# A hybrid decoder block on one core: both branch projections by seven products, the attention gate applied at the operand's load, transfers begun a set number of products ahead

## The chip, the core and the metric

The kernel runs on one core of a Trainium2 chip. The metric is the device time in microseconds, the median of several runs. Before the change it is 926.31 us (three runs, 925.58 to 927.93). A trace of one execution of the same kernel, taken by the hardware profiler, is what the numbers below are read from. Five engines work side by side, each through its own list of instructions in order: TensorE (PE, matrix products, with its weight loads listed as PEld), VectorE (DVE), ScalarE (ACT), GpSimd (POOL), and SyncE (SP). SP does no arithmetic here, it issues transfers; POOL issues the transfers of weights.

## What is computed

One layer, 1024 tokens, model width 1024, in float32. The reference, cut to what matters:

```python
h = rms_norm(x, norm_g[l])
proj = jnp.einsum("bsd,de->bse", h, w_in[l])
# u, g_rnn, q, k, v, g_attn, m_rnn, m_attn are column ranges of proj
u = causal_depthwise_conv(u, conv_w[l], conv_b[l])
y_rnn = rg_lru(u, ...) * jax.nn.silu(g_rnn)
y_attn = sliding_window_attention_with_sinks(q, k, v, attn_sinks[l]) * jax.nn.silu(g_attn)
merged = (jax.nn.sigmoid(m_rnn) * jnp.einsum("bsr,rd->bsd", y_rnn, w_rnn_out[l])
          + jax.nn.sigmoid(m_attn) * jnp.einsum("bsa,ad->bsd", y_attn, w_attn_out[l]))
x = x + jnp.einsum("bsd,de->bse", merged, w_o[l])
return rms_norm(x, final_norm_g)
```

The change is about the two projections in `merged`, each a 1024x1024 matrix times a 1024x1024 one.

## The kernel before

Everything is held feature by token: a tile is 128 features by 512 tokens (half of the sequence). TensorE works on a float32 operand that ACT and DVE have cut into a rounded high part and a remainder: ACT casts (`h`), DVE subtracts (`l`), which is `split_buf` (lines L422 and L423). One float32 product of a 128x128 block with a 128x512 tile is then three matmuls: high by high, high by low, low by high. This text calls them three rows of PE.

**Pairs and seven products.** A unit of 128 output features over all 1024 inputs is one column block of a weight. Two units form a pair, and a pair is a 2x2 block matrix A (A11, A12, A21, A22, each 512 inputs by 128 outputs) times the 2x2 block matrix B of the input (halves of the features by halves of the tokens). Class `Pair` computes it by the scheme of Strassen and Winograd with seven block products in place of eight. It needs sums of the blocks of A (S1 to S4, made on DVE for each pair), sums of the blocks of B (T1 to T4, made once for all pairs), a copy on ACT and five additions on DVE behind the products (L430). A block product is four blocks of 128 features by three matmuls, so 12 rows of PE. The projections of `w_in` (units `ug` for the recurrence and its gate, `mr` and `ma` for the merge gates, `k`, `v`, `q`, and `ga` for the attention gate) are done so.

**The two branch projections** (`zr` for the recurrence, `za` for attention, four pairs each) are done by `z_pair`, with eight products a pair: each of the two output blocks of a pair goes over eight feature blocks for both halves of the tokens. Their operand B comes from DRAM through `whole_from` (tiles `Wr`, cut into `Wh`, `Wl`). For `zr` it is `yr_dr`, written by the recurrence. For `za` it is `yg_dr`: `gate_attn` takes the silu of the gate (tile `tga`), loads the attention's result from `ya_dr` (tile `yld`), multiplies on DVE, and writes the product to `yg_dr`. Behind a pair, `z_pair` loads the stored merge gate (tile `tz`, from `tm_r` or `tm_a`), multiplies it with the result in PSUM (L999), and for `za` adds the two branches. Then `w_o` (`WO`, again `whole_from`) and the merged tiles (`mh`, `ml`) feed the last projection, the rows named `o`.

**What sets the order.** No engine's order is written out by hand. `Plan` collects all operations with costs, dependencies and priorities and lays them out by a list scheduler, engine by engine; table `TUNE` holds priorities, numbers of buffers by class, and in `orders` the order of pairs and of the 32 attention steps (`a00` to `a37`). A transfer may also be made to follow, in the plan, a key such as `first26` ("the pair with number 26 has begun"); such a key orders the plan, it is no semaphore on the chip. On the chip a transfer waits for its place in SP's or POOL's list, for its data, and for the buffer that it fills.

Of the kernel before, what the change touches and what calls it, by code (L numbers as in the profile page):

```python
# [17 lines left out]
S = 1024  # L18
D = 1024
P = 128  # L20
# [12 lines left out]
    'm': (30, 6, 3),  # L33
# [3 lines left out]
    'zy': 5,  # L37
    'raw': 5,
# [3 lines left out]
    'B': 23,  # L42
    'psw': 79,
    'psk': 0,
    'Y': 21,
    'ld': 8,
    'lds': 17,
    'kv': 8,
    'kvs': 4,
    'qt': 2,  # L50
    'qts': 8,
    'P': 13,
    'AO': 22,
# [12 lines left out]
    'xof': 153,
# [271 lines left out]
def hybrid_block_kernel(ctx: ExitStack, tc: tile.TileContext, x, wall, wo, bd, vec, gfin,  # L338
# [16 lines left out]
                "P": (16, 0, 0, TUNE["P"]), "AO": (32, 0, 0, TUNE["AOs"]), "Y": (64, 0, 0, TUNE["Y"]), "zy": (TUNE["zy"], 0, 0, 0), "wo": (32, 0, 0, TUNE["Y"]), "ld": (TUNE["ld"], 0, 0, TUNE["lds"]),  # L355
# [89 lines left out]


    class Pair:
# [38 lines left out]
        def product(self, ps, a, b, start):  # L486
            h, l = self.factor(a)
            for k in range(4):
                bh, bl = self.comb(b)[k]

                def go(k=k, bh=bh, bl=bl):
                    w = slice(k * P, (k + 1) * P)
                    kw = {} if start else {"skip_group_check": True}
                    nc.tensor.matmul(ps.t, h.t[:, w], bh.t, start=start and k == 0, stop=False, **kw)  # L494
# [3 lines left out]
                PE(go, 3, [h, l, bh, bl], [ps])  # L498

        def p1(self):  # L500
            self.a, self.c1 = bank("pair"), slot("p1")
            self.product(self.a, "A11", "B11", True)
            ACT(lambda q: q.copy(self.c1.t, self.a.t), HF, [self.a], [self.c1, f"first{self.i}"])

        def p2(self):
            self.product(self.a, "A12", "B21", False)

        def run(self):
            self.p1()
# [433 lines left out]
    yg_dr = dr.tile([KT, P, S], F32, name="yg_dr")  # L943

    def gate_attn(p, C):

        for q in range(2):
            for h in range(2):
                e_ = p + 4 * q
                src = C[q][h]  # L950
                t = slot("tga")
                ACT(lambda e, t=t, src=src: e.activation(t.t, src.t, AF.Silu), HF, [src], [t], tset=SILU)
                y = load("ld", "yld")
                DMA(lambda y=y: y.t, lambda e_=e_, h=h: ya_dr[e_, :, HALF[h]], 1 << 18,
                    [(ya_dr, (e_, n)) for n in range(4 * h, 4 * h + 4)], [y])
                tt(t, t, y, MUL)
                DMA(lambda e_=e_, h=h: yg_dr[e_, :, HALF[h]], lambda t=t: t.t, 1 << 18, [t], [(yg_dr, (e_, h))])

    def whole_from(src, after, prio, cls):

        T = {}

        def get(k, h):
            if (k, h) not in T:
                raw, hi, l = load("zy", "Wr"), buf(cls, dt=F32R, name="Wh"), buf(cls, dt=F32R, name="Wl")
                ap, key = src(k, h)
                DMA(lambda: raw.t, ap, 1 << 18, key + after, [raw], prio)
                split_buf(hi, l, raw, prio)
                T[k, h] = (hi, l)
            return T[k, h]  # L970

        return get

    MG = {}

    def z_pair(a, p, i, comb):

        for q, names in enumerate((("A11", "A12"), ("A21", "A22"))):
# [9 lines left out]
            for k in range(KT):  # L988
                h, l = W[k // 4]
                w = slice(k % 4 * P, k % 4 * P + P)  # L990
                for hf in range(2):
                    bh, bl = comb(k, hf)
                    PE(lambda ps=ps[hf], h=h, l=l, w=w, bh=bh, bl=bl, k=k: three(ps, h, l, w, bh, bl, k == 0, k == KT - 1), 3,
                       [h, l, bh, bl], [ps[hf], f"first{i}"])
            for hf in range(2):
                t = load("P" if a == "r" else "ld", "tz")
                DMA(lambda t=t: t.t, lambda e_=e_, hf=hf: tm_dr[a][e_, :, HALF[hf]], 1 << 18,
                    [(tm_dr[a], (e_, hf)), f"first{i - p}"], [t], TUNE["ztl"])
                DVE(lambda v, t=t, src=ps[hf]: v.scalar_tensor_tensor(t.t, t.t, 1.0, src.t, op0=ADD, op1=MUL), HF, [t, ps[hf]], [t])  # L999
                if a == "r":  # L1000
                    MG[e_, hf] = t
                else:
                    tt(MG[e_, hf], MG[e_, hf], t, ADD)

# [6 lines left out]
    ids = [base[a] + p for a, p in (it for it in seq if len(it) == 2)]  # L1011
    ZC = {}

    def begun(a, p):
        return f"first{base[a] + p}"

    def run_pair(a, p):
        i = ids.index(base[a] + p)
        if a[0] == "z":
            if p == 0:  # L1020
                ZC[a] = whole_from(dram_mat(yr_dr if a == "zr" else yg_dr), [begun(*TUNE[a])], TUNE["comb"], "Y")
            z_pair(a[1], p, ids[i], ZC[a])
            return
# [20 lines left out]
    def dram_mat(m):  # L1044
        return lambda k, h: ((lambda: m[k, :, HALF[h]]), [(m, (k, h))])
# [23 lines left out]
    WO = whole_from(lambda k, h: ((lambda: wo[k * P : (k + 1) * P, HALF[h]]), []), [begun(*TUNE["wo"])], TUNE["comb"], "wo")  # L1069
# [11 lines left out]
    for q in range(2):  # L1081
        DMA(lambda q=q: gf_b[q].t, lambda q=q: gfin[HALF[q]].partition_broadcast(P), 1 << 18, [begun(*TUNE["wo"])], [gf_b[q]])
    for r in range(NB):
        xh = [load("xo", "xo") for _ in range(2)]
        for c in range(2):
            DMA(lambda c=c, xh=xh, r=r: xh[c].t, lambda c=c, r=r: x[r * P : (r + 1) * P, HALF[c]], 1 << 18,
                [begun(*TUNE["wo"])], [xh[c]], TUNE["xof"])
# [77 lines left out]
```

## Time and profile before

| what | value |
|---|---|
| median of three runs | 926.31 us |
| the profiled execution's own time | 928.33 us |
| its span, first to last instruction | 926.6 us |
| mean granted clock of TensorE | 0.992 |
| last projection of `w_in` ends, first row of `zr` | 653.2 us, 653.45 us |
| last row of `za` begins | 832.2 us |
| last row of `o` begins | 919.39 us |

The page gives for each engine its busy time, its share of the span and its instructions. A group of instructions is one line of the kernel with the tiles that it writes and reads, a count, the busy time with the mean duration of one, and the idle time ahead of them with the releaser that ended it. The timeline lists instructions by start and duration. On PE and DVE, durations of instructions that follow each other overlap, so the cost of one in a stream is the step from start to start, not its duration.

### The profile page before, as it was taken

What the parts mean: (1) busy time and instruction counts of PE and PEld (TensorE: products, weight loads), DVE (VectorE), ACT (ScalarE), POOL (GpSimd) and SP (SyncE); (2) the same over time, 40 slices, a digit from 0 to 9 for tenths busy, and PEclk for the clock granted to TensorE, in tenths of its full rate; (3) what the DMA queues carried; (4) which work ended last, traced back from release to release, by engine and by line L of the source; (5) the groups of instructions that cost most, each with busy time, mean ns of one, the idle gap of its engine ahead of it and who ended that gap; (6) DMA issues with size and microseconds to landing.
All of it is one profiled execution on the core that took longest, in us unless ns stands there. A gap on an engine that the chain in (4) does not pass through costs nothing. (4 is left out here: it accounts for less than half of the span.)

```text
span 926.6 us, 13014 instructions
## 1 busy us (share of the span) xinstructions
PE 896.5 (97%) x4184; PEld 739.7 (80%) x4184; DVE 684.4 (74%) x1427; ACT 569.3 (61%) x1176; POOL 72.8 (8%) x131
## 2 busy tenths in 40 slices
PE   4999999999999999999999999999899999999996
PEld 3778888877888888788888788888688888888885
DVE  6987999989977889887898699789622533366433
ACT  7646999578658796969988888998511300133000
POOL 2101010001100100110001000001200010000000
PEclk9999999999999999999999999999999999999999
DMA  9311224616742345356555476438961284131111
GB/s 325 108 52 58 67 78 127 177 36 213 216 151 69 103 107 171 105 167 173 171 164 163 104 196 206 120 117 271 399 252 46 71 296 161 40 115 46 51 63 46
DMA packets 86884, 129.76 MB, mean 140 GB/s; under 512 B 10656, under 2 KB 40224, under 8 KB 86816
## 3 DMA queue, kind: packets, MB, share of 16 engines
q1 hardware_dynamic: 77216, 97.47, 33.4%
q0 software_dynamic: 9600, 31.46, 11.3%
q8 instruction: 33, 0.54, 0.2%
q14 instruction: 35, 0.29, 0.1%
HBM read 87.21 MB, written 41.68 MB: 139 GB/s over the span
## 5 line engine op out<-in xcount | busy, mean ns | idle before, releaser
L413 POOL DMA_DIRECT2D A<-in_wall_dram x120 | 64.4, 538 | 654.6 <-PE pair L496 111.1
L554 PE MATMUL z<-Wh,zh 128*128 128x512 f32 x256 | 100.5, 393 | 1.7 <-ACT Wh L422 1.6
L555 PE MATMUL z<-Wl,zh 128*128 128x512 f32 x256 | 100.4, 392 | 0.5 <-DVE Wl L423 0.5
L556 PE MATMUL z<-Wh,zl 128*128 128x512 f32 x256 | 100.3, 392 | 0.0
L999 DVE SCALAR_TENSOR_TENSOR tz<-tz,z 128x512 f32<-128x512 f32 x32 | 21.9, 686 | 98.0 <-PE z L556 95.4
L423 DVE TENSOR_TENSOR wl<-S,wh 128x512 fp32r<-128x512 f32 x96 | 65.3, 684 | 9.4 <-ACT wh L422 9.0
L422 ACT CAST Wh<-Wr 128x512 fp32r<-128x512 f32 x48 | 28.2, 619 | 66.8 <-PE z L555 31.5
L422 ACT CAST wh<-S 128x512 fp32r<-128x512 f32 x96 | 58.4, 616 | 9.6 <-DVE S L430 4.5
L900 ACT ACTIVATE sm<-sm,nm 128x256 f32<-128x256 f32 (+1 forms) x128 | 62.1, 489 | 0.0
L554 PEld LDWEIGHTS z<-Wh,zh 128*128 128x128 f32 x256 | 48.5, 189 | 12.6 <-ACT Wh L422 2.6
L555 PEld LDWEIGHTS z<-Wl,zh 128*128 128x128 f32 x256 | 48.5, 189 | 11.3 <-DVE Wl L423 1.2
L893 DVE CUSTOM_DVE_ANT_0 sm<-ps_s,mask_t,sink_t 128x256 f32<-128x256 f32 (+1 forms) x128 | 53.8, 459 | 4.9 <-PE ps_s L885 4.9
L422 ACT CAST mh<-tz 128x512 fp32r<-128x512 f32 x16 | 9.1, 618 | 78.2 <-DVE tz L430 78.2
L556 PEld LDWEIGHTS z<-Wh,zl 128*128 128x128 f32 x256 | 48.4, 189 | 10.0
L908 ACT ACTIVATE sm<-sm,dn 128x256 f32<-128x256 f32 (+1 forms) x128 | 53.3, 487 | 4.0 <-DVE dn L905 3.8
L549 ACT ACTIVATE sd<-ss,eps_t 128x1 f32<-128x1 f32 x16 | 4.3, 289 | 78.4 <-DVE ss L547 78.4
L423 DVE TENSOR_TENSOR wl<-A,wh 128x512 fp32r<-128x512 f32 x72 | 49.1, 682 | 4.5 <-ACT wh L422 4.5
L430 DVE TENSOR_TENSOR c<-pair,u 128x512 f32<-128x512 f32 x72 | 49.0, 682 | 3.7 <-PE pair L496 3.3
L555 PE MATMUL o<-Wl,mh 128*128 128x512 f32 x128 | 49.8, 389 | 0.0
L554 PE MATMUL o<-Wh,mh 128*128 128x512 f32 x128 | 49.8, 389 | 0.0
L556 PE MATMUL o<-Wh,ml 128*128 128x512 f32 x128 | 49.8, 389 | 0.0
L885 PE MATMUL ps_s<-K,qt 128*128 128x256 f32 (+1 forms) x288 | 43.4, 289 | 3.1 <-DMA qt<-st_q 2.6
(221 smaller groups left out, 2566.0 us busy)
## 6 DMA issues: line engine op xcount, KB each, us to landing
A<-in_wall_dram POOLq DMA_DIRECT2D x120, 256.0 KB, 3.5
qt<-st_q SPq DMA_DIRECT2D x32, 256.0 KB, 3.6
xt<-in_x_dram SPq DMA_DIRECT2D x16, 256.0 KB, 5.4
A<-in_wall_dram SPq DMA_DIRECT2D x16, 256.0 KB, 5.4
tm_r<-tm SPq DMA_DIRECT2D x16, 256.0 KB, 2.1
yr_dr<-tg SPq DMA_DIRECT2D x16, 256.0 KB, 2.1
K<-st_k SPq DMA_DIRECT2D x32, 128.0 KB, 3.5
st_q<-qh SPq DMA_DIRECT2D x32, 128.0 KB, 3.2
```

Of the source, the lines that this page charges most:

```text
L413: pl.op([("POOL", 1000.0)], reads, writes, lambda e: nc.gpsimd.dma_start(dst(), src()), prio, move=move)
L422: ACT(lambda e: e.copy(h(), src()), cols, reads, wh, prio)
L423: (DVE if psum else EW)(lambda e: e.tensor_tensor(l(), src(), h().bitcast(F32), op=ALU.subtract), cols, list(reads) + list(wh), wl, prio)
L430: (eng or EW)(lambda e: e.tensor_tensor(dst.t, a.t, b.t, op=op), HF, [a, b], [dst], prio)
L554: nc.tensor.matmul(ps.t, h.t[:, w], bh.t, start=start, stop=False)
L555: nc.tensor.matmul(ps.t, h.t[:, w], bl.t, start=False, stop=False)
L556: nc.tensor.matmul(ps.t, l.t[:, w], bh.t, start=False, stop=stop)
L885: nc.tensor.matmul(ps.t[:, j, o0 : o0 + pw], qt.t[:, h, :], K[m, half].t[:, c0 : c0 + pw], start=m == 0, stop=m == 1)
L893: DVE(lambda v, ps=ps, j=j, h=h, s=s: v.tensor_tensor_reduce(s.t[:, j, :], ps.t[:, j, :], att["mask"].t[:, 256 - w : 256], scale=-0.125, s ...
L900: ACT(lambda e, h=h, s=s, j=j: e.activation(s.t[:, j, :], s.t[:, j, :], AF.Exp, scale=-1.0, bias=nm.t[:, h : h + 1], accum_out=dn.t[:, h : ...
L908: ACT(lambda e, h=h, s=s, j=j: e.activation(s.t[:, j, :], s.t[:, j, :], AF.Identity, scale=dn.t[:, h : h + 1]), w, [(s, j), dn], [(s, j)], ...
L999: DVE(lambda v, t=t, src=ps[hf]: v.scalar_tensor_tensor(t.t, t.t, 1.0, src.t, op0=ADD, op1=MUL), HF, [t, ps[hf]], [t])
```

## The change

1. **Seven products for the branches.** `zr` and `za` go through `Pair` (in `z_seven`), as the other projections do. Their operands come from `comb_from`, which loads 16 raw tiles of a branch (class `Y`), makes T1 to T4 (16 subtractions on DVE), and cuts seven blocks of four tiles into high and low parts (28 casts, 28 subtractions), where `whole_from` cut 16 tiles.
2. **The attention gate at the load.** `gate_attn` takes the silu and writes it to a new array `sg_dr`; it no longer loads `ya_dr`, multiplies, or writes `yg_dr`. In its place `fetch` loads for each tile of `za`'s operand both `ya_dr` and `sg_dr` (tile `zg`, three buffers) and multiplies on DVE.
3. **Keys by products.** Every product of a pair now leaves a key ("product 217"), and transfers are ordered in the plan by a number of products ahead of the point of use: 21 ahead for the operands of `zr` and `za`, 11 for `w_o`, 3 for `x` and the final gain; the merge gates' tiles follow the pair's own seventh product.
4. **The table.** Priorities, buffer numbers and the order of pairs and attention steps are new. The attention begins earlier, `ga` and `ma` are spread differently, and `ma0` is the last pair ahead of `zr0`.

The core of the diff:

```diff
-    'zy': 5,
-    'raw': 5,
+    'zy': 7,
+    'zg': 3,
+    'raw': 4,
...
-    'zr': ('ga', 0),
-    'za': ('zr', 2),
-    'wo': ('za', 1),
-    'orders': 'ug6 ug4 ug2 k0 ug1 ug0 v0 q0 a00 ma1 ug7 mr3 ug3 q2 ug5 a01 a02 mr2 q1 a03 a04 a05 a06 '
-              'ma0 a07 a10 a11 a12 ma3 a13 a14 a15 a16 ma2 a17 a20 a21 a22 a23 q3 a24 a25 a26 a27 a30 '
-              'ga0 a31 a32 a33 ga1 a34 a35 a36 a37 ga2 ga3 zr0 zr1 zr2 zr3 za0 za1 za2 za3',
+    'gzr': 21,
+    'gza': 21,
+    'gwo': 11,
+    'gxo': 3,
+    'gt': -6,
+    'seven': 'ra',
+    'mgd': 0,
+    'orders': 'ug3 ug4 k0 ug5 ug7 q1 ug6 q0 ug0 ug1 v0 a00 mr3 a01 a02 mr2 a03 a10 a04 ug2 a11 a12 q2 '
+              'ma3 q3 a13 a05 a06 a14 ma1 a07 a15 a20 ma2 a21 a22 a16 a23 a24 a17 ga2 a30 a31 a25 ga1 '
+              'a32 a33 a34 a26 ga3 a35 a36 a27 a37 ga0 ma0 zr0 zr1 zr2 zr3 za0 za1 za2 za3',
...
-                y = load("ld", "yld")
-                DMA(lambda y=y: y.t, lambda e_=e_, h=h: ya_dr[e_, :, HALF[h]], 1 << 18,
-                    [(ya_dr, (e_, n)) for n in range(4 * h, 4 * h + 4)], [y])
-                tt(t, t, y, MUL)
-                DMA(lambda e_=e_, h=h: yg_dr[e_, :, HALF[h]], lambda t=t: t.t, 1 << 18, [t], [(yg_dr, (e_, h))])
+                DMA(lambda e_=e_, h=h: sg_dr[e_, :, HALF[h]], lambda t=t: t.t, 1 << 18, [t], [(sg_dr, (e_, h))])
+
+    def fetch(t, src, k, h, after, prio):
+
+        (ap, key), *more = src(k, h)
+        DMA(lambda: t.t, ap, 1 << 18, key + after, [t], prio)
+        for ap2, key2 in more:
+            g = load("zg", "zg")
+            DMA(lambda: g.t, ap2, 1 << 18, key2 + after, [g], prio)
+            tt(t, t, g, MUL, prio)
...
+            if n not in T:
+                a, b = {"T1": lambda: (raw("B12"), raw("B11")), "T2": lambda: (raw("B22"), right("T1")),
+                        "T3": lambda: (raw("B22"), raw("B12")), "T4": lambda: (raw("B21"), right("T2"))}[n]()
+                T[n] = [buf("Y", name=n) for _ in range(4)]
+                for k in range(4):
+                    tt(T[n][k], a[k], b[k], SUB, prio)
...
+    def z_seven(a, p, i, comb):
+        C = Pair(i, comb).run()
+        for q in range(2):
+            for hf in range(2):
+                z_tail(a, 2 * p + q, hf, C[q][hf], i)
```

How the lists of two engines change. The first place is the join of the two branches on DVE. Tiles named `zl` and `wl` are remainders of weights, `Wl` of the operand of `za` before, `B11l`, `T2l` and so on of the operand after; `tz` is a merge gate times a result. Before, from the last two gates of the third `zr` pair on:

```order
L999 SCALAR_TENSOR_TENSOR tz_7799<-tz_7799,z_7954 128x512
L999 SCALAR_TENSOR_TENSOR tz_7804<-tz_7804,z_7959 128x512
L423 TENSOR_TENSOR Wl_8059<-Wr_8023,Wh_8052 128x512
L423 TENSOR_TENSOR zl_8068<-A12_7887,zh_8057 128x512
L423 TENSOR_TENSOR Wl_8075<-Wr_8025,Wh_8066 128x512
L423 TENSOR_TENSOR Wl_8084<-Wr_8031,Wh_8079 128x512
L423 TENSOR_TENSOR Wl_8093<-Wr_8036,Wh_8088 128x512
L423 TENSOR_TENSOR Wl_8102<-Wr_8038,Wh_8097 128x512
```

Now, at the same place, from the addition that takes the last `zr` product out of PSUM (`c12`, which reads `pair_8271`) to the last remainder of the block T2 of `za`:

```order
L435 TENSOR_TENSOR c12_8364<-pair_8271,u2_8226 128x512
L428 TENSOR_TENSOR T2l_8371<-T2_8313,T2h_8322 128x512
L428 TENSOR_TENSOR T2l_8380<-T2_8327,T2h_8373 128x512
L428 TENSOR_TENSOR wl_8389<-A22_8188,wh_8387 128x512
L1032 SCALAR_TENSOR_TENSOR tz_8334<-tz_8334,pair_8143 128x512
L1032 SCALAR_TENSOR_TENSOR tz_8338<-tz_8338,c12_8364 128x512
L1032 SCALAR_TENSOR_TENSOR tz_8343<-tz_8343,c21_8332 128x512
L435 TENSOR_TENSOR S4_8405<-A12_8200,S2_8263 128x512
L1032 SCALAR_TENSOR_TENSOR tz_8352<-tz_8352,c22_8303 128x512
L428 TENSOR_TENSOR T2l_8410<-T2_8336,T2h_8382 128x512
L428 TENSOR_TENSOR T2l_8414<-T2_8345,T2h_8412 128x512
```

The operand of `za` was cut here in single remainders ahead of the rows that need them; now the last remainders of T2 stand behind an addition that waits for the last `zr` product, and behind four gate products. From `c12_8364` to the first weight remainder of the second `za` pair (`wl_8472`) the list has 25 rows. On PE, between the last row of `pair_8271` and the first row of the second `za` pair (`pair_8478`), stand three products, 36 rows.

The second place is SP's list where the operand of `zr` is loaded. `yg_dr` and `sg_dr` are the gate's arrays, `yld` the loads that the gate no longer makes, `qt` a query tile of the attention. Before:

```order
L411 DMA yg_dr_81<-tga_6882 128x512
L411 DMA Wr_7378<-yr_dr_78 128x512
L411 DMA yg_dr_81<-tga_6891 128x512
L411 DMA Wr_7393<-yr_dr_78 128x512
L411 DMA Wr_7409<-yr_dr_78 128x512
L411 DMA yld_7411<-ya_dr_80 128x512
L411 DMA yld_7422<-ya_dr_80 128x512
L411 DMA Wr_7432<-yr_dr_78 128x512
```

Now:

```order
L416 DMA qt_6804<-st_q3_91 128x4x128
L416 DMA sg_dr_81<-tga_6816 128x512
L416 DMA sg_dr_81<-tga_6823 128x512
L416 DMA YB22_6846<-yr_dr_78 128x512
L416 DMA sg_dr_81<-tga_6839 128x512
L416 DMA ya_dr_80<-y_6851 64x4x128
L416 DMA YB12_6864<-yr_dr_78 128x512
L416 DMA YB12_6877<-yr_dr_78 128x512
```

The loads of `yr_dr` stood among the gate's loads and stores after the last attention step; now 12 of the 16 stand among the last attention steps' own transfers, and the last four ahead of the final store of `sg_dr`.

More of the change, by code (lines that the diff above doesn't have):

```diff
@@ L444, in col, with mark, ahead @@
         return vec_t.t[:, i : i + 1]
+    POS = {}
+    def mark(i, n):
+        return f"product {7 * POS[i] + n}"
+    def ahead(i, n):
+        return f"product {7 * i - n}"
     class Pair:
@@ L484, in factor, with product @@
             return self.W[a]
-        def product(self, ps, a, b, start):
+        def product(self, n, ps, a, b, start):
             h, l = self.factor(a)
@@ L941, in attn_values @@
             [y], [(ya_dr, (2 * g + b, n)) for b in range(2)], run=512, issue=650.0)
-    yg_dr = dr.tile([KT, P, S], F32, name="yg_dr")
+    sg_dr = dr.tile([KT, P, S], F32, name="sg_dr")
     def gate_attn(p, C):
@@ L972, in whole_from, with comb_from, raw, right @@
         return get
-    MG = {}
+    def comb_from(src, after, prio):
+        C, Y, T = {}, {}, {}
+        def raw(n):
+            q, h = {"B11": (0, 0), "B12": (0, 1), "B21": (1, 0), "B22": (1, 1)}[n]
+            if n not in Y:
+                Y[n] = [load("Y", "Y" + n) for _ in range(4)]
+                for k in range(4):
+                    fetch(Y[n][k], src, k + 4 * q, h, after, prio)
+            return Y[n]
+        def right(n):
+            if n[0] == "B":
+                return raw(n)
+            if n not in T:
+                a, b = {"T1": lambda: (raw("B12"), raw("B11")), "T2": lambda: (raw("B22"), right("T1")),
+                        "T3": lambda: (raw("B22"), raw("B12")), "T4": lambda: (raw("B21"), right("T2"))}[n]()
+                T[n] = [buf("Y", name=n) for _ in range(4)]
+                for k in range(4):
+                    tt(T[n][k], a[k], b[k], SUB, prio)
+            return T[n]
+        def get(n):
+            if n not in C:
+                xs = right(n)
+                C[n] = [(buf("B", dt=F32R, name=n + "h"), buf("B", dt=F32R, name=n + "l")) for _ in range(4)]
+                for k in range(4):
+                    split_buf(*C[n][k], xs[k], prio)
+            return C[n]
+        return get
+    MG = {}
+    zm_dr = dr.tile([KT, P, S], F32, name="zm_dr")
+    def z_tail(a, e_, hf, src, first):
+        first = ahead(POS[first], TUNE["gt"])
+        t = load("P" if a == "r" and not TUNE["mgd"] else "ld", "tz")
+        DMA(lambda: t.t, lambda: tm_dr[a][e_, :, HALF[hf]], 1 << 18, [(tm_dr[a], (e_, hf)), first], [t], TUNE["ztl"])
+        DVE(lambda v: v.scalar_tensor_tensor(t.t, t.t, 1.0, src.t, op0=ADD, op1=MUL), HF, [t, src], [t])
+        if a == "r" and TUNE["mgd"]:
+            DMA(lambda: zm_dr[e_, :, HALF[hf]], lambda: t.t, 1 << 18, [t], [(zm_dr, (e_, hf))])
+        elif a == "r":
+            MG[e_, hf] = t
+        else:
+            if TUNE["mgd"]:
+                MG[e_, hf] = load("P", "mg")
+                DMA(lambda: MG[e_, hf].t, lambda: zm_dr[e_, :, HALF[hf]], 1 << 18, [(zm_dr, (e_, hf)), first], [MG[e_, hf]], TUNE["ztl"])
+            tt(MG[e_, hf], MG[e_, hf], t, ADD)
+    def z_seven(a, p, i, comb):
[3 more added lines that the diff above has]
+                z_tail(a, 2 * p + q, hf, C[q][hf], i)
     def z_pair(a, p, i, comb):
@@ L993, in z_pair @@
                     PE(lambda ps=ps[hf], h=h, l=l, w=w, bh=bh, bl=bl, k=k: three(ps, h, l, w, bh, bl, k == 0, k == KT - 1), 3,
-                       [h, l, bh, bl], [ps[hf], f"first{i}"])
+                       [h, l, bh, bl], [ps[hf]] + [mark(i, 4 * q + k // 2)] * (hf == 0 and k % 2 == 0 and 4 * q + k // 2 < 7))
             for hf in range(2):
[L996 to L1003, printed above, removed]
+                z_tail(a, e_, hf, ps[hf], i)
     st_k, st_q = {}, {}
@@ L1011, in hybrid_block_kernel @@
     ids = [base[a] + p for a, p in (it for it in seq if len(it) == 2)]
+    POS.update({u: i for i, u in enumerate(ids)})
     ZC = {}
-    def begun(a, p):
-        return f"first{base[a] + p}"
     def run_pair(a, p):
@@ L1042, in run_pair, with yr_part, ya_part @@
         pl.bias = 0
-    def dram_mat(m):
-        return lambda k, h: ((lambda: m[k, :, HALF[h]]), [(m, (k, h))])
+    def yr_part(k, h):
+        return [((lambda: yr_dr[k, :, HALF[h]]), [(yr_dr, (k, h))])]
+    def ya_part(k, h):
+        return [((lambda: ya_dr[k, :, HALF[h]]), [(ya_dr, (k, n)) for n in range(4 * h, 4 * h + 4)]),
+                ((lambda: sg_dr[k, :, HALF[h]]), [(sg_dr, (k, h))])]
     prev = []
```

79 lines of the change are left out of this document (41 added, 38 removed).

## The prediction

> **What bounds the kernel now.** I read the page's first block and groups, then PE's timeline, the windows, and the waits at the places these name.
>
> ```profile
> span 926.6 us, 13014 instructions
> PE 896.5 (97%) x4184; PEld 739.7 (80%) x4184; DVE 684.4 (74%) x1427; ACT 569.3 (61%) x1176; POOL 72.8 (8%) x131
> L554 PE MATMUL z<-Wh,zh 128*128 128x512 f32 x256 | 100.5, 393 | 1.7 <-ACT Wh L422 1.6
> L555 PE MATMUL z<-Wl,zh 128*128 128x512 f32 x256 | 100.4, 392 | 0.5 <-DVE Wl L423 0.5
> L556 PE MATMUL z<-Wh,zl 128*128 128x512 f32 x256 | 100.3, 392 | 0.0
> ```
>
> PE is busy for 97% of the span; the branch projections are 3 x 256 = 768 of its rows, with almost no idle time ahead of them. A mean of 393 ns isn't what a row costs, since rows overlap. The step is read at the first rows of three products that follow each other:
>
> ```profile
> 641.31 0.39 PE L494 MATMUL pair<-T3h,wh 128*128 128x512 f32 x1
> ...
> 644.03 0.39 PE L494 MATMUL pair<-T1h,wh 128*128 128x512 f32 x1
> ...
> 646.75 0.39 PE L494 MATMUL pair<-T4h,wh 128*128 128x512 f32 x1
> ```
>
> A product of 12 rows takes 2.72 us, 0.227 us a row. Next the windows; columns are PE, PEld, DVE, ACT and POOL busy, the granted clock, the DMA share and GB/s:
>
> ```profile
> 600.00:625.00 25.00, 24.94 (x146) 21.45 (x146) 21.14 (x65) 23.07 (x62) 2.14 (x4) 1.00 0.37 108
> 625.00:650.00 25.00, 24.63 (x113) 19.85 (x111) 22.77 (x40) 20.31 (x40) 4.59 (x9) 1.00 0.85 276
> 650.00:675.00 25.00, 22.23 (x86) 17.11 (x87) 16.19 (x26) 13.79 (x25) 5.57 (x11) 0.93 1.04 399
> 675.00:700.00 25.00, 25.00 (x112) 20.71 (x111) 4.46 (x7) 3.53 (x6) 0.54 (x1) 1.00 0.54 194
> 825.00:850.00 25.00, 25.00 (x112) 20.71 (x111) 22.30 (x40) 12.36 (x23) 0.00 (x0) 1.00 0.19 63
> ```
>
> Up to 650 us PE is full while DVE has some 3 us idle in 25. Through the branch projections DVE is nearly idle (4.46 us of 25 at 675). So every stage is bound by PE, and the stage that is changed has spare DVE time. One spot breaks this, 650 to 675: PE 22.23, transfers at 399 GB/s. There the first `zr` pair waits for its operand:
>
> ```profile
> 661.61 0.39 PE L554 MATMUL z<-Wh,zh 128*128 128x512 f32 x1
> ...
> 665.62 0.50 PE L554 MATMUL z<-Wh,zh 128*128 128x512 f32 x1 [1.57 <-ACT Wh L422]
> 666.35 0.52 PE L555 MATMUL z<-Wl,zh 128*128 128x512 f32 x1 [0.23 <-DVE Wl L423]
> 666.69 0.60 PE L556 MATMUL z<-Wh,zl 128*128 128x512 f32 x1
> ...
> 670.08 0.42 PE L555 MATMUL z<-Wl,zh 128*128 128x512 f32 x1
> 670.34 0.39 PE L556 MATMUL z<-Wh,zl 128*128 128x512 f32 x1
> ```
>
> From 661.61 to 670.34 are 17 rows: 8.73 us where 17 x 0.227 = 3.9 would do, a loss of 4.9. Of it 1.6 us are no waits: the eight steps from 666.69 to 670.08 take 0.42 us each, a lowered clock (0.93 in that window).
>
> **The change, part by part.**
>
> *PE.* Eight pairs lose one product of eight: 8 x 2.72 = **-21.8 us**. The lists agree: 4184 matmuls before, 4088 now.
>
> *DVE and ACT.* A pair adds 4 sums, 3 remainders and 5 additions on DVE, 12 x 8 = 96; a branch adds 16 subtractions and 12 remainders, 28 x 2 = 56: together 152 rows. ACT gains 3 casts and a copy a pair and 12 casts a branch, 56 rows. Their steps, from streams of nine and of eight:
>
> ```profile
> 835.38 5.51 DVE L423 TENSOR_TENSOR ml<-tz,mh 128x512 fp32r<-128x512 f32 x9
> 840.81 0.69 DVE L430 TENSOR_TENSOR xo<-o,xo 128x512 f32<-128x512 f32 x1
> ...
> 834.76 4.26 ACT L422 CAST mh<-tz 128x512 fp32r<-128x512 f32 x8
> ```
>
> A DVE row costs (840.81 - 835.38) / 9 = 0.60 us, an ACT row 4.26 / 8 = 0.53. That is 152 x 0.60 = 91 us more on DVE (684.4 becomes some 776) and 30 us on ACT. Beside PE there is room on average, but not everywhere. From the first row of `ma0` to the first row of the second `za` pair, PE's list has 456 rows, 456 x 0.227 = 103.5 us; DVE's in the same stretch 177 rows, 106 us. DVE enters without a lead, as it has additions to take from the products just ahead. So DVE, not PE, sets the end of this stretch, and it shows at the join of the branches: from `c12_8364`, which can't start before the last `zr` product ends, to `wl_8472`, which the second `za` pair needs, stand 25 DVE rows, 15.0 us. PE has three products there, 8.2 us. PE waits for the difference, **+6.8 us**. Behind the join PE has 300 rows to the first `o` row, 68 us, and DVE 107 rows, 64 us: the loss isn't made up, since PE is full again, but it doesn't grow. ACT's 30 us lie beside this: it uses 4 to 14 us of 25 there.
>
> *The start of `zr`.* Its operand is loaded ahead of three whole pairs (21 products, 57 us), 12 of 16 tiles among the last attention steps. The loss of **-4.9 us** goes. What is late next is the addition behind the last `w_in` pair, which stays.
>
> *Slow rows at the join.* The waits there are of the same size as those at 661.61, split over some 13 us. Ends: 0, or twice the 1.6 us above; I take one such stretch, **+1.6 us**. The Trainium skill ("TensorE: Matmul & The Clock Gate", section "What's actually happening") has the clock lowered only after an idle window of about 3.4 us. The rows above speak against it as a bound: the longest single wait was 1.57 us and eight slow steps followed. By the page this term would be 0 and the sum 907.3.
>
> *The gate at the load.* Transfers stay the same in number: 16 stores to `yg_dr` become 16 to `sg_dr`, 16 loads `yld` and 16 of `yg_dr` become 16 of `ya_dr` and 16 of `zg`. The 16 multiplications move from the gate's stage into the stretch above and are in its 177 rows. New are DVE rows that wait for loads: a freed buffer lets SP issue, and, by the buffer that each transfer waits for, the row that uses the tile stands 9 to 16 rows later in DVE's list (9 for most `tz`), 5.4 us at least. The nearest rows, issue to landing:
>
> ```profile
> yld<-ya_dr SPq DMA_DIRECT2D x16, 256.0 KB, 4.1
> tz<-tm_r SPq DMA_DIRECT2D x16, 256.0 KB, 6.3
> Wr<-yg_dr SPq DMA_DIRECT2D x16, 256.0 KB, 2.6
> DVE tz L999 <- DMA tz<-tm_r: 2.5, 1, 2.5
> ```
>
> At 2.6 or 4.1 us nothing waits; at 6.3 each of some five rounds through these buffers is 0.9 late, 4.5 us. A gain is excluded, since no DVE wait for `yld` is among the waits. The loads are now spread, not in a burst at 399 GB/s, so I take the row of 4.1 with one late round, **+0.9 us**. What queues behind such a row on DVE is everything, and PE behind it.
>
> *Loads of `x`, `w_o` and the merge gates, begun late.* 29 transfers of 256 KB stand together in SP's list some 15 us ahead of `o`: 7.6 MB, 19 us at 399 GB/s. The last `w_o` tiles are needed some 25 us into `o`. Nothing; if they land at half that rate, up to 5 us.
>
> *The new table up to 600 us.* The same pairs and attention steps in another order. PE's waits that it could change:
>
> ```profile
> PE ps_s L885 <- DMA qt<-st_q: 2.6, 2, 1.9
> PE pair L494 <- DVE c L430: 2.0, 4, 1.0
> ```
>
> With four query buffers for two the 2.6 may go; as much may come elsewhere. I take 0, ends -3 and +3.
>
> **Sum.** -21.8 - 4.9 + 6.8 + 1.6 + 0.9 = -17.4. The profiled execution took 928.33 us, 2.0 above the median of the three runs, 926.31; so 910.9 for its like, and **909 us** for the median.
>
> **Rivals.**
>
> *The join is filled.* If DVE gains a lead ahead of `ma0` (it has 3 us idle in 25), its rows are done before PE asks. Then 6.8 + 1.6 fall away: 900.5. Against it: 177 rows for 456, and `c12_8364` can't be early.
>
> *No slow rows at the join.* 907.3, within the forecast's own range. For it: each wait is short. Against: 666.69 to 670.08. It is the result that the Trainium skill's rule, named above, leads to.
>
> *DVE waits on others too.* Rounds at 6.3 us cost 4.5; and remainders wait for ACT's casts:
>
> ```profile
> DVE wl L423 <- ACT wh L422: 13.5, 19, 1.7
> ```
>
> 13.5 us over 24 pairs cost nothing where DVE had slack; for eight pairs where it has none it is 4.5. With a second slow stretch: 909 - 0.9 + 4.5 + 4.5 + 1.6 = 918.7.
>
> *Slower: the rounds of loads set the pace.* The chain of waits has one landing much longer than the medians above:
>
> ```profile
> 647.35 9.37 DMA yg_dr<-tga
> ```
>
> From the first gate multiplication on, DVE would go at the speed of free buffer, issue, landing, use: five rounds of (landing - 5.4). At 9.4 us that is 20 us, with a second slow stretch 909 - 0.9 + 20 + 1.6 = 929.7. It decides from a landing of 8.7 us; 9.3 make it slower than can be mistaken. Against it: the medians of 2.6 to 6.3.
>
> *That PE doesn't do less* is excluded by its list.
>
> **How the numbers follow.** The forecast with its own range, 904 to 914 (the ends of the slow rows, and -3 to +3): 0.55, of which 0.2 for the rival without slow rows. The join filled, below 904: 0.20. DVE waits too, 914 to 923.5: 0.16. Between 923.5 and 929.1, a landing near 9: 0.05. Slower still: 0.04. A measurement can tell some 0.3% from no change, 2.8 us. So faster 0.91, same 0.05, slower 0.04. The range that leaves out 0.06 below and 0.12 above is 899 to 920.
>
> **What would show it.** PE's products of `zr` and `za` with 672 rows at 0.227; no wait and no clock below 1.00 at the first `zr` product; DVE over 22 us of 25 busy from some 600 us to the join; PE waiting for `T2l`, `B21l` and `wl` of DVE at the join, 5 to 9 us in all, and hardly elsewhere in these stages; `zg` landing in 3 to 5 us. Wrong would be PE waiting at every `zr` or `za` product, or waits for `zg` and `tz` at the head of DVE's waits.

## The result, and the profile after

| kernel | median | lowest to highest | runs | ratio to before, 95% interval |
|---|---|---|---|---|
| before | 926.61 us | 925.58 to 927.93 | 4 | |
| changed | 901.26 us | 899.97 to 902.15 | 4 | 0.9725, 0.9707 to 0.9742 |

The change makes the kernel 25.4 us faster. The forecast was 909 us with a range of 899 to 920, so the time lies in the range, 8 us below the forecast. The profiled execution took 901.53 us with a span of 899.8, where the prediction's sum had 910.9 for an execution like that of before.

The page of the changed kernel first, its line of engines:

```profile
span 899.8 us, 13035 instructions
PE 874.7 (97%) x4088; PEld 721.8 (80%) x4088; DVE 774.4 (86%) x1579; ACT 599.9 (67%) x1232; POOL 72.9 (8%) x131
```

DVE is busy for 774.4 us (776 was forecast), ACT for 599.9 (30.6 more, 30 forecast). PE is still at 97%. Where the time went is read from three points of PE's timeline: the first row of `zr`, the first row of `o`, and the end of the span. The rows of the changed kernel, then the one of before that isn't in the prediction:

```profile
644.67 0.39 PE L508 MATMUL pair<-B11h,wh 128*128 128x512 f32 x1
...
805.60 0.39 PE L568 MATMUL o<-Wh,mh 128*128 128x512 f32 x1
```

```profile
832.41 0.39 PE L554 MATMUL o<-Wh,mh 128*128 128x512 f32 x1
```

| stage | before | after | difference |
|---|---|---|---|
| up to the first `zr` row | 653.45 us | 644.67 us | -8.8 |
| branches, to the first `o` row | 179.0 us | 160.9 us | -18.0 |
| `o` and the end of the span | 94.2 us | 94.2 us | 0 |

The branches gave 18.0 us, where the prediction's terms for them sum to 17.4. The other 8.8 us come from ahead of the branches, where PE's work is the same in both kernels and the prediction had 0. The stages are those of two single executions and sum to 26.8 us, where the medians differ by 25.4: the profiled execution of before took 928.33 us, 1.7 above its median, that of the changed kernel 0.3 above. So a stage is good to some 1.5 us.

Next the windows of the changed kernel, with columns as in the prediction:

```profile
500.00:525.00 25.00, 25.00 (x150) 21.74 (x149) 19.66 (x70) 24.04 (x75) 1.61 (x3) 1.00 0.42 107
...
650.00:675.00 25.00, 25.00 (x112) 20.62 (x111) 24.97 (x42) 13.90 (x26) 1.61 (x3) 1.00 0.62 194
675.00:700.00 25.00, 25.00 (x111) 20.37 (x110) 24.23 (x41) 4.44 (x8) 1.60 (x3) 1.00 0.71 228
...
725.00:750.00 25.00, 21.69 (x75) 16.08 (x74) 25.00 (x43) 13.38 (x25) 2.15 (x4) 0.80 0.12 35
```

From 650 to 700 DVE has hardly a gap, 24.97 and 24.23 of 25 us, where it had 16.19 and 4.46 before. PE is full at the start of `zr` (22.23 before) and short in one window only, 725 to 750, with a clock of 0.80. That is the join. PE's timeline there:

```profile
721.11 0.39 PE L508 MATMUL pair<-B11h,wh 128*128 128x512 f32 x1
...
727.47 0.50 PE L509 MATMUL pair<-T2l,wh 128*128 128x512 f32 x1 [1.89 <-DVE T2l L428]
...
729.32 0.80 PE L508 MATMUL pair<-B21h,wh 128*128 128x512 f32 x1 [0.30 <-ACT B21h L427]
730.48 0.79 PE L509 MATMUL pair<-B21l,wh 128*128 128x512 f32 x1 [0.36 <-DVE B21l L428]
731.07 0.63 PE L510 MATMUL pair<-B21h,wl 128*128 128x512 f32 x1
...
732.88 0.80 PE L509 MATMUL pair<-B21l,wh 128*128 128x512 f32 x1 [0.76 <-DVE B21l L428]
...
738.95 0.40 PE L508 MATMUL pair<-B11h,wh 128*128 128x512 f32 x1
```

From 721.11 to 738.95 are 42 rows, 17.84 us where 42 x 0.227 = 9.5 would do: a loss of 8.3 us, against 6.8 + 1.6 = 8.4 forecast. The waits are only 3.3 us of it. The rest are rows with a step of 0.43 us in place of 0.227. Beside it DVE's timeline, first and last the addition that takes the last `zr` product and the weight remainder that the second `za` pair needs (`c12_8364` and `wl_8472` in the prediction):

```profile
721.31 0.69 DVE L435 TENSOR_TENSOR c<-pair,u 128x512 f32<-128x512 f32 x1
...
727.93 1.90 DVE L435 TENSOR_TENSOR YB<-YB,zg 128x512 f32<-128x512 f32 x3
...
731.53 0.69 DVE L435 TENSOR_TENSOR YB<-YB,zg 128x512 f32<-128x512 f32 x1
...
735.75 0.69 DVE L428 TENSOR_TENSOR wl<-A,wh 128x512 fp32r<-128x512 f32 x1
```

That is 14.4 us from the start of the first to the start of the last of the 25 rows, 24 steps of 0.60, and 15.1 us to the end of the last; 15.0 were forecast. DVE takes the addition 0.2 us behind the start of PE's first `za` row, so it isn't late there; the work queued behind it is what PE waits for, four of the gate's multiplications (`YB<-YB,zg`) among it.

The loads, issue to landing:

```profile
zg<-sg_dr SPq DMA_DIRECT2D x16, 256.0 KB, 3.7
...
tz<-tm_r SPq DMA_DIRECT2D x16, 256.0 KB, 3.9
```

And the waits of PE, of the changed kernel and then those of before that the prediction didn't show:

```profile
PE pair L508 <- DVE c L435: 0.8, 2, 0.5
```

```profile
PE pair L494 <- DVE y L939: 0.9, 1, 0.9
PE psb L728 <- DVE ul L423: 0.5, 1, 0.5
...
PE ps_s L885 <- DVE nm L893: 0.5, 1, 0.5
...
PE ptp L919 <- ACT sm L908: 0.2, 1, 0.2
500.00:525.00 25.00, 23.15 (x128) 19.70 (x127) 18.97 (x70) 19.95 (x62) 1.07 (x2) 0.93 0.50 142
```

Waits that run through the pairs and the attention came to 2.6 (`qt`) + 2.0 (`c`) + 0.9 + 0.5 + 0.5 + 0.2 = 6.7 us before, and 0.8 are left. Of the 2.0 for `c`, 0.98 us at 650.61 are the wait behind the last `w_in` pair, which the prediction expected to stay; it went too. Behind the longest wait, 1.85 us for `qt` at 512.00, the clock fell to 0.93 in its window, some 0.07 x 25 = 1.8 us. Together 6.7 - 0.8 + 1.8 = 7.7 of the 8.8 us. What removed them was open: the new order, the new numbers, or the gate's work that left this stage.

### The profile page after: what moved, and what is told of

Read it like the earlier page. It is cut to its first block, busy times and chain, and to the rows that moved or that the text cites. A ratio compares the mean times of both kernels' runs of the same rounds, so it can differ in the third digit from the quotient of the medians.

```text
span 899.8 us, 13035 instructions
## 1 busy us (share of the span) xinstructions
PE 874.7 (97%) x4088; PEld 721.8 (80%) x4088; DVE 774.4 (86%) x1579; ACT 599.9 (67%) x1232; POOL 72.9 (8%) x131
## 4 chain that ended last, share of the span: by engine, by line
PE 63%; DVE 3%; ACT 3%; issue 1%; DVEq 0%
PE pair L508 15%; PE pair L509 15%; PE pair L510 15%; PE o L569 3%; PE o L570 3%; PE o L568 3%; PE ps_s L899 3%; PE ptp L933 3%; PE po L947 1%; PE po L946 1%; ACT sm L914 1%; ACT sm L922 1%; DVE wl L428 1%; DVE cu L728 0%; ACT ph L427 0%
## 5 line engine op out<-in xcount | busy, mean ns | idle before, releaser
L427 ACT CAST wh<-A 128x512 fp32r<-128x512 f32 x96 | 59.3, 617 | 12.1 <-PE pair L510 6.3
L509 PE MATMUL pair<-B21l,wh 128*128 128x512 f32 x128 | 51.2, 400 | 1.1 <-DVE B21l L428 1.1
L508 PE MATMUL pair<-B11h,wh 128*128 128x512 f32 x128 | 51.7, 404 | 0.5 <-DVE B12l L424 0.5
L508 PE MATMUL pair<-B21h,wh 128*128 128x512 f32 x128 | 51.9, 406 | 0.3 <-ACT B21h L427 0.3
L508 PE MATMUL pair<-B22h,wh 128*128 128x512 f32 x128 | 51.0, 398 | 0.8 <-DVE c L435 0.8
L510 PE MATMUL pair<-B21h,wl 128*128 128x512 f32 x128 | 50.9, 398 | 0.0
L508 PE MATMUL pair<-T3h,wh 128*128 128x512 f32 x128 | 50.7, 396 | 0.0
L508 PE MATMUL pair<-T4h,wh 128*128 128x512 f32 x128 | 50.7, 396 | 0.0
L508 PE MATMUL pair<-T1h,wh 128*128 128x512 f32 x128 | 50.6, 396 | 0.0
L509 PE MATMUL pair<-B11l,wh 128*128 128x512 f32 x128 | 50.5, 394 | 0.0
```

Of the source, the lines that this page charges most:

```text
L427: ACT(lambda e: e.copy(h(), src()), cols, reads, wh, prio)
```

## The experiments

"The numbers" are the entries of the table that both kernels have, apart from `orders`. All ratios are to the kernel before on the same chip. Its medians beside the runs are 926.6 to 927.1 us, so differences between the times of two runs carry some 0.5 us of that.

**Is the join DVE's total work, or what stands behind one addition?** The first kernel keeps the plan and leaves out the 16 gate multiplications, so attention's branch lacks its gate.

```diff
-            tt(t, t, g, MUL, prio)
+            EW(lambda e: None, HF, [t, g], [t], prio)
```

> The changed kernel with its plan unchanged, but the 16 multiplications of the attention's result with the gate are left out of DVE's list (the loads of both stay), so the attention branch is projected without its gate. Theory A, the waits at the join come from what stands behind the addition that takes the last zr product out of PSUM: of its 25 rows 4 go, 2.4 us; the wait for T2l (1.89 us) stays, as none of the 4 stands ahead of it; 897 to 899.5 us. Theory B, DVE is late by the time it enters the join because it is full from 600 us on: 16 rows, 9.6 us, are more than the 8 us lost there, T2l's wait goes too and the clock stays at 1.00; 892 to 894 us.

Measured: 898.36 us, ratio 0.9687 (0.9672 to 0.9701). Its waits of PE and a window:

```profile
PE pair L509 <- DVE T2l L428: 1.9, 1, 1.9
```

```profile
675.00:700.00 25.00, 25.00 (x112) 20.72 (x111) 18.23 (x30) 5.08 (x9) 1.61 (x3) 1.00 0.69 229
```

DVE now has 6.8 us idle in the window, and PE's longest wait at the join is the same 1.9 us. Taking 16 x 0.60 = 9.6 us from DVE won 2.9, and 4 x 0.60 = 2.4 of it are the four multiplications that stand behind the addition at 721.31. The rows behind that addition set the join; the time that DVE gained ahead of it is idle. That speaks against the rival of the prediction in which a lead of DVE fills the join.

**The same multiplications on GpSimd.**

```diff
-            tt(t, t, g, MUL, prio)
+            pl.op([("POOL", 1245.0)], [t, g], [t], lambda e, t=t, g=g: nc.gpsimd.tensor_tensor(t.t, t.t, g.t, op=MUL), prio)
```

> The changed kernel with the 16 gate multiplications on GpSimd in place of DVE, about 1.3 us each there. If GpSimd works beside DVE without touching it, DVE is relieved as when the rows are left out: 897 to 900 us, and DVE's step stays 0.60 us. If the two get in each other's way, the 20 us of GpSimd work show as longer DVE rows in 640 to 735 us, and the gain is given back: 901 to 906 us.

Measured: 910.7 us, ratio 0.9821 (0.9806 to 0.9835). That is 9.4 us slower than the changed kernel, worse than either expectation. The group of the multiplications, GpSimd's first three of them, and DVE's rows beside these:

```profile
L976 POOL TENSOR_TENSOR YB<-YB,zg 128x512 f32<-128x512 f32 x16 | 29.1, 1848 | 13.3 <-DMA zg<-sg_dr 6.8 <-DVE S L435 4.0 <-DMA YB<-ya_dr 2.5
```

```profile
654.57 8.09 POOL L976 TENSOR_TENSOR YB<-YB,zg 128x512 f32<-128x512 f32 x3 [3.95 <-DVE S L435]
```

```profile
658.63 1.18 DVE L435 TENSOR_TENSOR S<-A,S 128x512 f32<-128x512 f32 x1
659.73 1.77 DVE L435 TENSOR_TENSOR T<-YB,T 128x512 f32<-128x512 f32 x1
661.43 1.78 DVE L428 TENSOR_TENSOR wl<-A,wh 128x512 fp32r<-128x512 f32 x1
663.13 0.68 DVE L435 TENSOR_TENSOR c<-pair,u 128x512 f32<-128x512 f32 x1
```

Three rows of GpSimd took 8.09 us, 2.7 each, where the shortest of the 16 took 1.25. DVE's rows up to 658.03 kept their 0.68 us although the group had begun; the three behind them took 1.18 to 1.78 us. The row after those, which reads PSUM and starts after GpSimd's end, is back at 0.68. The longest stretch came with the second group, 3.3 us for two rows:

```profile
668.27 3.73 POOL L976 TENSOR_TENSOR YB<-YB,zg 128x512 f32<-128x512 f32 x3
```

```profile
668.54 4.62 DVE L428 TENSOR_TENSOR T4l<-T,T4h 128x512 fp32r<-128x512 f32 x2
```

There GpSimd's three rows took some 1.25 us each, and DVE alone was held up. Estimated against steps of 0.60, DVE's rows from 640 to 760 us were stretched by 13 us in all, more than the 9.6 that it gave away. PE then waited 5.0 us for `T4l` and 4.5 for `T2l`. The plan was laid out anew around the moved rows, so a part of the 9.4 us may be their new places; this wasn't separated. The Trainium skill ("SBUF — State Buffer", section "Who interferes with whom") says that a DVE instruction with two SBUF inputs contends with a GpSimd instruction that reads SBUF, as the second input comes through an interface that both share. The rows above agree: in the first group both engines stretch, in the second DVE alone.

**Seven products for `zr` alone.**

```diff
-    'seven': 'ra',
+    'seven': 'r',
```

> Seven products for the recurrence branch, eight for the attention branch; gate at the load and table as changed. Theory A and B alike (PE's rows set the time, the join costs 8): za gains four products, 4 x 2.72 = 10.9 us, and its operand is cut in 16 remainders in place of 28 plus 16 differences, so the join's 8.2 us go: 901.3 + 10.9 - 8.2 = 904 us. Rival, DVE sets the time of the whole stage: with 28 + 4 x 12 = 76 DVE rows fewer (46 us) it is no slower than 901, perhaps 895.

Measured: 904.76 us, ratio 0.9757 (0.9743 to 0.9772), as expected. The windows at the join:

```profile
725.00:750.00 25.00, 24.06 (x105) 19.19 (x104) 16.71 (x27) 6.13 (x11) 1.07 (x2) 1.00 0.67 237
750.00:775.00 25.00, 25.00 (x112) 20.71 (x111) 8.96 (x14) 3.33 (x6) 0.00 (x0) 1.00 0.20 64
```

The slow clock is gone and DVE is idle again. Four products cost 4 x 2.72 = 10.9 us, the join no longer loses its 8.3, and a wait of 0.9 us for `Wl` comes in its place: +3.5, where 904.76 - 901.26 = 3.5 were measured. So the second half of the change, seven products for `za`, is worth only 3.5 us, as the join eats most of its gain.

**Who brought the 8.8 us?** One number first. Buffers for the query tiles in the kernel before:

```diff
-    'qt': 2,
+    'qt': 4,
```

> The kernel before with four query buffers in place of two, nothing else by hand; the planner re-sorts around it. If PE's waits for query tiles (2.6 us, and the slow rows behind the longer one, some 1.7 us) are what the new table saved ahead of the branches: 922 us, and no wait for qt. Rival, the order of attention and pairs saved it: 925 to 930 us, waits only change their names.

Measured: 940.04 us, ratio 1.014 (1.0115 to 1.0165), slower than either expectation. PE's wait for `qt` fell from 2.6 to 1.5 us, but its waits for `c` rose to 3.6, for `pw` to 1.7 and for `sm` to 1.5: a number of buffers that is changed lays out the whole plan anew. This run settles nothing about the 8.8 us. The next three set back whole parts of the table in the changed kernel: the order alone, the numbers alone, and both.

```diff
-    'orders': 'ug3 ug4 k0 ug5 ug7 q1 ug6 q0 ug0 ug1 v0 a00 mr3 a01 a02 mr2 a03 a10 a04 ug2 a11 a12 q2 '
+    'orders': 'ug6 ug4 ug2 k0 ug1 ug0 v0 q0 a00 ma1 ug7 mr3 ug3 q2 ug5 a01 a02 mr2 q1 a03 a04 a05 a06 '
...
```

> The changed kernel with the order of pairs and attention steps of before, all new numbers kept. What is open: the first zr row came 8.8 us earlier than before (644.7 us for 653.5 in the profiles), with the same products ahead of it, and PE's waits between 40 and 650 us fell from 7.7 to 1.6 us. Theory A, the order brings it: first zr row at 651 to 654, PE's waits up to there 6 to 8 us, 908 to 911 us in all. Rival B, the numbers (buffers and how far ahead each stage is planned) bring it: first zr row at 644 to 647, waits 1.5 to 4 us, 901 to 904 us in all. I lean to B, as the waits that went were for the query buffers and for DVE's additions, which the numbers set.

> The changed kernel with the shared numbers of before (buffers, how far ahead each stage is planned), the new order and the new entries kept. Theory A, the order brought the 8.8 us ahead of zr: first zr row near 645, 901 to 904 us. Rival B, the numbers did: first zr row at 651 to 654 and at least 908 to 911 us. More than that, 912 to 930 us, if the old numbers also fit the rest of the changed program badly: additions and remainders for za that now come with 152 rows more on DVE, and the last loads ahead of o; PE would then wait at the join for longer than 8.2 us or at the start of o (86.8 us in both profiles so far), and that would say nothing of the 8.8 us. I lean to this last.

> The changed kernel with order and shared numbers of before: seven products, the gate at the load and loads begun by products, without the new table. Theory: the table is worth at least the 8.8 us ahead of zr, 908 to 911 us, with the first zr row at 651 to 654. Rival: the moved gate brought them (16 loads and 16 stores less among the attention steps' last ones), so that the first zr row stays near 645, 901 to 904 us. If old_numbers comes out above 912, this one does as well, by the same waits.

| kernel | median | ratio, 95% interval | first `zr` row | branches |
|---|---|---|---|---|
| before | 926.6 us | | 653.45 us | 179.0 us |
| changed | 901.26 us | 0.9725 (0.9707 to 0.9742) | 644.67 us | 160.9 us |
| old_order | 902.63 us | 0.9738 (0.9721 to 0.9755) | 646.24 us | 159.9 us |
| old_numbers | 936.84 us | 1.0109 (1.0089 to 1.0129) | 654.66 us | 185.4 us |
| old_table | 934.21 us | 1.0077 (1.0055 to 1.0099) | 653.51 us | 184.6 us |

In the new code the numbers bring nearly all of it; the order is worth 1.6 us. The join of old_order shows one thing more. From 732.76 us on its steps are back at 0.23 us, and PE then waits for the weight remainder of the second `za` pair:

```profile
738.18 0.50 PE L508 MATMUL pair<-B11h,wl 128*128 128x512 f32 x1 [1.06 <-DVE wl L426]
```

The 42 rows of the join, from 722.80 to 739.21, lose 6.9 us there, against 8.3 in the changed kernel.

And with the old numbers the changed code is **slower than before**, by 1.1% and 0.8%, though it has 96 rows of PE less. In old_table the branches take 184.6 us, 5.6 more than with eight products. PE's timeline of old_table shows the greatest loss, and DVE's what stood ahead:

```profile
808.69 0.39 PE L507 MATMUL pair<-B21l,wh 128*128 128x512 f32 x1
822.11 0.80 PE L508 MATMUL pair<-B21h,wl 128*128 128x512 f32 x1 [13.03 <-DVE wl L426]
```

```profile
805.95 0.69 DVE L433 TENSOR_TENSOR c<-pair,u 128x512 f32<-128x512 f32 x1 [2.82 <-PE pair L508]
806.55 0.68 DVE L1030 SCALAR_TENSOR_TENSOR tz<-tz,pair 128x512 f32<-128x512 f32 x1
...
816.55 0.69 DVE L433 TENSOR_TENSOR tz<-tz 128x512 f32<-128x512 f32 x1
817.16 0.68 DVE L433 TENSOR_TENSOR u<-pair,p 128x512 f32<-128x512 f32 x1
817.76 3.69 DVE L426 TENSOR_TENSOR ml<-tz,mh 128x512 fp32r<-128x512 f32 x6
821.37 0.68 DVE L426 TENSOR_TENSOR wl<-A,wh 128x512 fp32r<-128x512 f32 x1
```

DVE first waits for PE, 2.82 us for a product. Then it does the gate products of two whole pairs with their additions, one more addition and six remainders for `o`, 15 us of work that PE doesn't wait for here, and the weight remainder that PE stands still for is behind them. DVE wasn't out of time, for it stood idle for 2.03 and 2.82 us just ahead; the order of its list is what costs. So the numbers are no ornament of this change but the part that places 152 added DVE rows. No run takes the moved gate or the keys by products back alone, so what these two are worth by themselves isn't shown.

**The numbers without the change.** The kernel before with those new numbers that bear on pairs and attention, 16 entries:

```diff
-    'm': (30, 6, 3),
+    'm': (29, 2, 3),
...
-    'qt': 2,
-    'qts': 8,
-    'P': 13,
+    'qt': 4,
+    'qts': 1,
+    'P': 17,
...
-    'prep': 183,
-    'att': 0,
+    'prep': 256,
+    'att': 73,
...
```

> The kernel before with those new numbers that bear on the pairs and the attention steps (m, raw, B, psw, ld, lds, qt, qts, P, lru0, prep, att, val, gate, lru, qk), its own order, eight products and the gate before the load; the numbers of the branch stages stay. Theory, these numbers alone brought the 8.8 us ahead of zr: first zr row at 645 to 648, 918 to 921 us in all if the branches take the 179 us that they took. Rival, they do it only where the gate's 16 loads, 16 multiplications and their waits are out of the attention stage: first zr row at 651 to 655, 924 to 930 us. I lean to the theory by little, as the changed kernel with the order of before had its first zr row at 646.2.

Measured: 921.29 us, ratio 0.9944 (0.9923 to 0.9965). Its waits of PE and its window:

```profile
PE pair L494 <- DVE c L430: 1.8, 3, 1.3
PE po L933 <- DVE pw L423: 1.3, 3, 0.6
```

```profile
500.00:525.00 25.00, 25.00 (x139) 21.11 (x139) 20.82 (x66) 24.41 (x72) 1.61 (x3) 1.00 0.57 156
```

The first `zr` row is at 648.48, between the two expectations. Of the 8.8 us, 5.0 come from these numbers in the old code and the old order: the wait for `qt` and the slow clock behind it are gone. Going on to old_order wins 2.2 more, and the new order 1.6. The 2.2 lie between two kernels that differ in the change's code and in the numbers of the branches; the wait of 1.3 us for an addition ahead of the last product of `w_in`, which is in this kernel and not in old_order, is the largest piece seen of it. What brings the rest wasn't separated. The numbers reach into the start of `zr` as well: here the branches take 176.3 us, to the first `o` row at 824.74, where the kernel before took 179.0, with the loads begun as before. So 2.7 of the 4.9 us lost there can go without the earlier loads.

Two single numbers at last, one in each kernel:

```diff
-    'att': 0,
+    'att': 73,
```

> The kernel before with one number set to that of the new table: attention steps yield 73 places in the plan to other work ('att'). PE's waits of before between 40 and 650 us were mostly in the attention stage (2.6 for qt, 2.0 for additions, 0.9 for y). Theory, this number is what thins them: 2 to 4 us less up to the first zr row, 922 to 925 us. Rival, as with the query buffers, one number moved by itself re-sorts the plan and costs more than it wins: 930 to 942 us.

Measured: 923.47 us, ratio 0.9967 (0.9956 to 0.9978), with the first `zr` row at 650.18, as the theory had it: some 3 us less. This entry makes attention steps yield to other work in the plan.

```diff
-    'qt': 4,
+    'qt': 2,
```

> The changed kernel with two query buffers for four, one number of the table set back. The kernel before waited 2.6 us for qt, and the lower clock behind it cost some 1.7 more. Theory, the buffers took these away: waits for qt of 2 to 3 us come back between 480 and 620 us, first zr row at 648 to 650, 904.5 to 906 us in all. Rival, the new plan loads the queries early enough in two: no wait for qt over 0.5 us, within 1 us of 901.3.

Measured: 903.16 us, ratio 0.975 (0.9728 to 0.9771), the first `zr` row at 646.99. PE has no wait for `qt` among its waits, so the theory's mechanism falls, yet 2.3 us are lost ahead of `zr`, more than the rival had. With two buffers the plan is another one and PE waits elsewhere, 0.7 us for `nm` as the longest new wait; where the rest of the 2.3 us went wasn't separated.

**A version that fills the join.** If DVE's rows behind the last `zr` product are the trouble, PE needs work there that asks less of DVE. The first `za` pair goes by eight products, straight from the four blocks of the operand; T1 to T4 are first needed by the second pair, 22 us later.

```diff
+            if a == "za" and p == 0:
+                part = {(0, 0): "B11", (0, 1): "B12", (1, 0): "B21", (1, 1): "B22"}
+                z_pair("a", p, ids[i], lambda k, h: ZC["za"](part[k // 4, h])[k % 4])
+                return
```

> The changed kernel, but the first of the four za pairs by eight products, straight from B11, B12, B21 and B22; the other seven pairs of the branches by seven as they were. PE gets 12 rows more (2.7 us) and four whole-operand products that need no difference of the operand, while DVE still makes the differences T1 to T4, which the second za pair needs 22 us later. Theory, the 8.2 us at the join are DVE's lag behind the first za pair and nothing else: they go, no PE wait over 0.5 us from 721 to 740, clock 1.00; 901.3 - 8.2 + 2.7 = 895.8, up to 899.5 if T4l comes some us late for the second pair (54 DVE rows at 0.60 behind the last zr product in the changed kernel, 74 here: 44 us for some 41 us of PE). Rival, DVE's lag only moves: PE waits for T4l or wl of the second pair as long as it did at the join, slow rows included, and the product comes on top: 901.3 + 2.7 = 904.

Measured: 903.37 us, ratio 0.9747 (0.973 to 0.9764). The window from 725 to 750 has PE at 25.00 of 25 and the clock at 1.00, so the join's loss is gone. It came back in two other places, read from the window of the first, then from PE's and ACT's timelines:

```profile
675.00:700.00 25.00, 22.32 (x91) 17.47 (x90) 22.83 (x39) 4.63 (x8) 1.61 (x3) 0.93 0.66 221
```

```profile
690.70 0.50 PE L508 MATMUL pair<-B21h,wh 128*128 128x512 f32 x1 [2.02 <-ACT wh L427]
...
802.15 0.51 PE L510 MATMUL pair<-T3h,wl 128*128 128x512 f32 x1 [1.40 <-DVE wl L428]
```

```profile
690.03 0.62 ACT L427 CAST wh<-A 128x512 fp32r<-128x512 f32 x1 [3.44 <-DMA A<-in_wall_dram]
```

At 690 a weight tile landed late, and slow rows followed (clock 0.93 in that window). Whether this was a rule or an accident of the plan was the question of the last run: one number, by which the preparation of factors yields to the operand's.

```diff
-    'prep': 256,
+    'prep': 280,
```

> The kernel with the first za pair by eight products again, and one number beside it: the preparation of a pair's factor yields 280 places in the plan for 256, so that it stands behind the first uses of za's operand and the load of a factor tile that came 3.4 us late for ACT at 690 us has another place. There the run before it gave back what it had won at the join: waits of 2.0 and 0.7 us at 690, 1.4 us at 802, and slow rows behind each. Theory: the join's 8.2 us were won and these are accidents of the plan; without them 901.3 - 8.2 + 2.7 = 895.8, so 895 to 898 us, and no PE wait over 0.5 us between the first zr row and o. Rival: DVE has no lead to give anywhere in these stages, so whatever leaves one place waits in the next: 901 to 904 us, with waits for wl or T4l of 4 us or more elsewhere in zr and za.

Measured: 896.16 us (895.95 to 896.66), ratio 0.9673 (0.9652 to 0.9693): 895.8 was worked out. The windows from the join on:

```profile
725.00:750.00 25.00, 25.00 (x112) 20.71 (x111) 24.86 (x42) 11.45 (x22) 1.75 (x4) 1.00 0.16 46
750.00:775.00 25.00, 25.00 (x110) 20.03 (x109) 24.90 (x41) 9.59 (x17) 0.92 (x2) 1.00 0.28 87
```

Both engines are full at once. With eight products in one pair and this number the kernel is 5.1 us faster than with seven, and it beats both of those compared. That the join's loss went by the eight products is seen in za0_eight, which has the old 256. What 280 does with seven products in every pair wasn't run, so the 5.1 us belong to the two edits together.

## Why the prediction was right, and where it was off

- **PE, -21.8 us.** Right. With 2.72 us a product, 64 products are 174.1 of the 179.0 us of the branches before, and 56 are 152.3 of the 160.9 after; the rest are losses, 4.9 and 8.6 us.
- **The start of `zr`, -4.9.** Right: all of it went. At the first `zr` product there is no wait and the window's clock is 1.00. That the earlier loads alone did it isn't shown, as before_att_numbers lost 2.7 us less there without them.
- **The join, +6.8 and +1.6.** Right in place, cause and sum, 8.3 us. The sign that it named, 5 to 9 us of waits there, didn't come: the waits are 3.3 us, and slow rows take the other 5.0. The split into prices still holds by an estimate from the rows above. DVE ends the remainder for the second pair at 735.75 + 0.69 = 736.44; with rows at 0.227 PE would have stood before it until then, and the 42 rows would have ended near 737.4, a loss of 6.8. The slow rows carried PE past that point without a wait, to 738.95, 1.5 us later. old_order bears this out: with rows back at 0.23 us, PE waits for that remainder and loses 6.9 us. no_mult and seven_r_only show the cause, za0_eight and za0_eight_prep that PE's own work can cover it.
- **The gate at the load, +0.9.** Too high by 0.9. `zg` landed in 3.7 us and `tz` in 3.9, the medians within the 5.4 that the lists give, and no DVE row that takes one of them waited for its load.
- **Loads of `x` and `w_o`, 0.** Right, 94.2 us from the first `o` row on, as before.
- **The new table up to 600 us, 0 with ends of -3 and +3.** This is the term that was mis-sized: it measured -8.8, and it makes up nearly the whole difference of the forecast. The bound was taken from one wait of 2.6 us. All waits that the pairs and the attention had come to 6.7 us, and the window from 500 to 525 has a clock of 0.93 besides; both were in the profile of before, and a lower end of -8.5 could have been read from them. The value 0 wasn't unreasonable by itself: the table with one number changed moved the other way, to 940.04, and its old form in the new code gains nothing there.
- **The rivals.** The join filled was to give 900.5; the time came close to that, but by another way, as the join lost its 8.3 us. By the sum and its own ends, 904 to 914, the time is outside; it lies in the range of 899 to 920 because that reached down for this rival, which didn't happen. That part of the agreement is luck. Waits of DVE on loads, and rounds of loads as the pace, weren't seen. What the prediction lacked is the case that old_table shows: the same code, with DVE's rows in a worse order, ends at 934.21. The slower side had a price, but on the loads and not on DVE's order.

On the clock the Trainium skill ("TensorE: Matmul & The Clock Gate", section "What's actually happening") was the source of a rival without slow rows, for it names an idle window of about 3.4 us. This trace doesn't agree with that as a condition: no wait at the join was longer than 1.89 us, and steps of 0.43 us followed up to 738.60.

## What to carry to other kernels

When products are saved at the price of additions on another engine, compare the two engines' lists over each stretch between the points where one has to wait for the other, and not over the whole kernel: here the second half of the saving was worth 3.5 us of 10.9. At such a point the dearer form of the product can be the faster one, if it asks less of the engine that is behind and the plan around it leaves it room: za0_eight took 903.37 us, slower than the 901.26 with seven products, and with one number more 896.16. And where a planner lays out the code, price the plan's own waits ahead of the change, all of them and the slow clock behind them, as what a new set of numbers may take away or add.

## What the runs showed of the hardware

- A GpSimd multiplication of 128x512 beside DVE rows with two inputs took 1.85 us on average (1.25 the shortest, 4.69 the longest), and single DVE rows 1.18 to 4.02 us for 0.68, the longest one of the two at 668.54. Moving 16 rows off DVE, 9.6 us of its time, made the kernel 9.4 us slower.
- At the join the clock fell with waits of 1.89, 0.30, 0.36 and 0.76 us within some 7 us, none of them long, and from 731.07 to 738.60 PE's steps between these waits were 0.43 us in place of 0.227.
